# Normalisation and half of the offsets at a feed-forward's entry: from ScalarE to VectorE

## The chip, the core and the metric

The kernel runs on one core of a Trainium2 chip. The metric is the time of one execution on the device in microseconds, the median of several runs. In what follows PE is TensorE (PEld its weight loads), DVE is VectorE, ACT is ScalarE, POOL is GpSimd and SP the queue that issues most transfers. L200 is line 200 of the kernel before; the changed kernel's lines stand three or four further down in the parts that matter (L405 of before is L408 of after).

## What is computed

Two layers of an encoder over 512 tokens of 1024 channels, each a half-step feed-forward, a mixer of four groups of attention heads, and another half-step feed-forward, with a layer norm behind each:

```python
alpha = (2 * DEPTH) ** 0.25
for l in range(DEPTH):
    x = _layer_norm(alpha * x + 0.5 * _swiglu(x, ffn_w_gu[l, 0], ffn_w_down[l, 0]), ln_g[l, 0], ln_b[l, 0])
    mix = _token_mixers(x, w_in[l], ...)
    x = _layer_norm(alpha * x + mix, ln_g[l, 1], ln_b[l, 1])
    x = _layer_norm(alpha * x + 0.5 * _swiglu(x, ffn_w_gu[l, 1], ffn_w_down[l, 1]), ln_g[l, 2], ln_b[l, 2])
```

`_layer_norm` subtracts the mean, multiplies by 1 / sqrt(variance + 1e-5), then applies a gain and an offset for each channel. `_swiglu(h)` is (silu(h W_gate) * (h W_up)) W_down with 2816 inner columns. All is float32.

## The kernel before

The tokens are handled in four blocks of 128 (t = 0 to 3). Every float32 matrix product is made of three products of rounded operands: each operand is split into a high part (a copy in the rounded type, made on ACT) and a low part (the operand less its high part, made on DVE), and high x high, high x low and low x high are added up in PSUM.

The gate and up products of a feed-forward use a 2x2 block scheme with seven products instead of eight. It wants sums and differences of the blocks of both operands. On the side of x these are al1 to al7, each of 8 x 256 turned values (channels by tokens), each again as a high and a low part. Blocks 0 and 1 of the tokens give al1 and al2; blocks 2 and 3, combined with what was kept of 0 and 1, give al5, al7, al6, al4 and al3, by way of the differences t5, t7, t6 and t3 (L216, L218, L220, L225). On the side of the weights, the columns come in pairs (`Pair`). A pair has a step for each product: step 1 (al1, PSUM tile ga) and step 2 (al2, gb), then `rest`: step 5 (al5, gc), 6 (al6, ga), 7 (al7, ga), 3 (al3, gc) and 4 (al4, ga). Its weight sums are made in place on DVE: b11+b12 (L458), t2 (L468), b12+b22 (L476) and b21+t2 (L491); `parts4` then splits a sum or a weight into wh (ACT, L404) and wl (DVE, L405).

`norm_to_al` is the entry to a feed-forward. It runs three times: at the end of the mixer of layer 0, at the seam between the layers (after the second feed-forward of layer 0), and at the end of the mixer of layer 1. For each block it adds the accumulated product to x (L349), takes the statistics (L350, L331), forms the factor 1 / sqrt on DVE and POOL (L333, L334), forms minus mean times factor on DVE (L352), and normalises the block's two halves of 128x512 on ACT (L354), as factor times x plus that. Then `to_al` turns the block: PE transposes it (L112) into two PSUM tiles xtp of four 128x128 pieces, g = 0 for the lower 512 channels and g = 1 for the upper. In the turned x a channel is a partition, so `whole` applies the layer norm's gain and offset with one ACT operation for each piece (L200), eight for a block. For blocks 0 and 1 the results are kept (ac) and split at once into al1 (g = 0) and al2 (g = 1), by ACT (L181) and DVE (L182) with the sign turned; for blocks 2 and 3 they are t7 (g = 0) and a22 (g = 1), from which t5 and the rest follow (splits on L178, L179, L181, L182). The x that is not turned gets its gain and offset later, out of the way (`gain_later`).

A PSUM tile xtp comes free when its four pieces have been read, and there are two of them.

The order on each engine is made by a scheduler from priorities; the normalisation stands at a raised priority (`tc.high_priority(NORMS)`). Each engine then runs its own list in order, and waits on semaphores where an operand or a buffer is not ready.

Of the kernel before, what the change touches and what calls it, by code (L numbers as in the profile page):

```python
# [14 lines left out]
AF = mybir.ActivationFunctionType  # L15
ALU = mybir.AluOpType
# [57 lines left out]
def tile_encoder(ctx: ExitStack, tc: tile.TileContext, d: dict, out: bass.AP):  # L74
    nc = tc.nc
    ve, se, ge, te = nc.vector, nc.scalar, nc.gpsimd, nc.tensor
# [18 lines left out]
    def load(dst, src):  # L95
        nc.sync.dma_start(dst, src)
# [39 lines left out]
    def turned_x(t, gs=range(2)):  # L136

        for g in gs:
            b = bank4("pt", "xtp")
            for k in range(4):  # L140
                tr(b[:, k], x[t][:, (4 * g + k) * P:(4 * g + k + 1) * P])
            yield g, b
# [29 lines left out]
    def al_split(n, i, src, sign=1.0):  # L172

        for h, l, k0, nk in al[n]:
            cs = slice(i * P, (i + 1) * P)
            v = src[:, k0:k0 + nk]
            if sign == 1.0:
                se.copy(h[:, :, cs], v)  # L178
                ve.tensor_tensor(l[:, :, cs], v, h[:, :, cs].bitcast(F32), op=ALU.subtract)  # L179
            else:  # L180
                se.activation(h[:, :, cs], v, AF.Copy, scale=sign)  # L181
                ve.scalar_tensor_tensor(l[:, :, cs], v, sign, h[:, :, cs].bitcast(F32), op0=ALU.mult, op1=ALU.subtract)  # L182

    def b4(tag, name):
        return block(tag, name).rearrange("p (t c) -> p t c", c=P)

    def to_al(t, gt=None, gs=range(2)):


        i = t % 2  # L190

        def whole(g, b, tag, name):

            o = b4(tag, name)
            if gt is None:
                se.copy(o, b)
                return o, o
            for k in range(4):
                kk = 4 * g + k
                se.activation(o[:, k], b[:, k], AF.Identity, bias=gt[:, 1, kk:kk + 1], scale=gt[:, 0, kk:kk + 1])  # L200
            return o, o

        if t < 2:
            for g, b in turned_x(t, gs):
                kept[g, i], b = whole(g, b, "hl", "ac")
                al_split(1 + g, i, b, -1.0)
            return
        turned = list(turned_x(t))
        a22, b1 = whole(*turned[1], "tb", "a22")
        if gt is None:  # L210
            b0 = turned[0][1]
            t7 = b4("tb", "t7")
        else:
            t7, b0 = whole(*turned[0], "tb", "t7")
        t5 = b4("tb", "t5")
        ve.tensor_tensor(t5, b0, a22, op=ALU.subtract)  # L216
        al_split(5, i, t5)
        ve.tensor_tensor(t7, b0, kept[0, i], op=ALU.subtract)  # L218
        t6 = kept[0, i]
        ve.tensor_tensor(t6, t6, t5, op=ALU.subtract)  # L220
        al_split(6, i, t6)
        al_split(7, i, t7)
        al_split(4, i, b1, -1.0)
        t3 = kept[1, i]
        ve.tensor_tensor(t3, t3, t6, op=ALU.subtract)  # L225
        al_split(3, i, t3)
# [71 lines left out]
    def gain_tiles(l, i, tags=("hl",) * 4):  # L298

        out_ = []  # L300
        for n in range(2):
            for w in ("ln_g", "ln_b"):
                t = block(tags[len(out_)], w)
                load(t, d[w][l, i, n * FD:(n + 1) * FD].partition_broadcast(P))
                out_.append(t)
        return out_
# [22 lines left out]
    def norm_factors(stt):  # L329
        mv = sm.tile([P, 2], F32, tag="mv", name="mv", bufs=2)  # L330
        ve.bn_aggr(mv, stt)  # L331
        rs = sm.tile([P, 2], F32, tag="rs", name="rs", bufs=2)
        ve.tensor_scalar(rs[:, 0:1], mv[:, 1:2], 1.0, EPS * INV_A * INV_A, op0=ALU.mult, op1=ALU.add)  # L333
        ge.tensor_tensor(rs[:, 1:2], rs[:, 0:1], mhalf[:, 0:1], op=ALU.pow)  # L334
        return rs, mv
# [3 lines left out]
    def norm_to_al(t, accs, c, l, i):  # L339

        if t == 0:
            gt = sm.tile([P, 2, 8], F32, tag="gt", name="gt", bufs=1)
            load(gt, d["ln_t"][l, i])
            gained[:] = [gt]
        with tc.high_priority(NORMS):
            stt = sm.tile([P, 2, 6], F32, tag="bn", name="bn", bufs=2)
            xs = [x[t][:, n * FD:(n + 1) * FD] for n in range(2)]
            for n in range(2):
                ve.scalar_tensor_tensor(xs[n], accs[n], c * INV_A, xs[n], op0=ALU.mult, op1=ALU.add)  # L349
                ve.bn_stats(stt[:, n], xs[n])  # L350
            rs, mv = norm_factors(stt)
            ve.tensor_scalar(rs[:, 0:1], mv[:, 0:1], rs[:, 1:2], -1.0, op0=ALU.mult, op1=ALU.mult)  # L352
            for n in range(2):
                se.activation(xs[n], xs[n], AF.Identity, bias=rs[:, 0:1], scale=rs[:, 1:2])  # L354
        to_al(t, gained[0])

        if t == NT - 1:
            gained.append(gain_tiles(l, i, ("tb", "tb", "tb", "hl")))
# [478 lines left out]
    def mixer(l):  # L837
# [795 lines left out]
        def finish(t, accs):  # L1633
            norm_to_al(t, accs, 1.0, l, 1)
# [24 lines left out]
    for l in range(DEPTH):  # L1659
        ffn(l, 0, False, (new_xT, to_xT), ("p", "oT" if l else "nat"))  # L1660
        mixer(l)
        ffn(l, 1, l == DEPTH - 1, (norm_to_al,) if l < DEPTH - 1 else None)
# [24 lines left out]
```

## Time and profile before

| what | value |
|---|---|
| timed runs | 1926.14 us median of 3 (1925.88 to 1926.17) |
| the profiled execution | 1928.49 us, of which the span is 1926.7 us |
| mean granted TensorE clock | 0.988 |
| normalisations on ACT (L354) | 24 of 128x512 |
| offsets on ACT (L200) | 96 of 128x128, of which 48 write ac |
| L352 on DVE | 12 |
| entry at the mixer's end, layer 0 | about 607 to 648 us |
| entry at the seam between the layers | about 955 to 994 us |
| entry at the mixer's end, layer 1 | about 1560 to 1601 us |

A profile shows when each engine was busy. An engine's idle time matters only where another engine waits for its result, so the shares of the whole span say less than the windows of single stages. "x<-y" in a row names the tile written and the tiles read; a duration is that of one operation, and since operations in a queue overlap, the distance from start to start can be shorter.

### The profile page before, as it was taken

The numbers are of one execution on the slowest core, as the hardware profiler recorded it, in microseconds if no ns is written. First come the engines' busy times: TensorE is split into PE (matmuls) and PEld (weight loads), VectorE is DVE, ScalarE is ACT, GpSimd is POOL, SyncE is SP. The second block draws the span as 40 slices with busy tenths as digits, with TensorE's granted clock in tenths as the row PEclk, the third lists the DMA queues.
The fourth block names the chain that finished last, engine by engine and source line by source line (L and its number), as shares of the span: only waits on it lengthen the run. The fifth ranks groups of instructions, "written<-read, shape, count | busy, mean of one in ns | idle before, by whom it ended". The sixth has DMA issues, their size and how long they took to land.

```text
span 1926.7 us, 32397 instructions
## 1 busy us (share of the span) xinstructions
PE 1875.4 (97%) x12252; PEld 1704.4 (88%) x12252; DVE 1696.6 (88%) x2739; ACT 1061.6 (55%) x1851; POOL 251.6 (13%) x381
## 2 busy tenths in 40 slices
PE   7999999999999999999999999999999989999998
PEld 7999998888887899999789999988887879999996
DVE  7999995858988999999599999958689989999975
ACT  5555554248776645555375555532587865455551
POOL 0000000245731000000000000002467300000001
PEclk9999999999999999999999999999999999999999
DMA  6333314243343424233342333241533335144221
GB/s 231 107 121 108 102 52 136 81 121 99 93 105 110 138 94 131 84 104 112 108 133 80 106 99 121 65 144 52 144 92 84 102 110 170 50 132 131 64 91 66
DMA packets 164701, 205.65 MB, mean 107 GB/s; under 512 B 15360, under 2 KB 123904, under 8 KB 164544
## 3 DMA queue, kind: packets, MB, share of 16 engines
q1 hardware_dynamic: 164544, 203.57, 34.3%
q8 instruction: 97, 1.59, 0.3%
q14 instruction: 60, 0.49, 0.1%
HBM read 178.49 MB, written 2.10 MB: 94 GB/s over the span
## 4 chain that ended last, share of the span: by engine, by line
PE 63%; DVE 9%; ACT 2%; POOL 1%; DMA 1%; issue 1%; SPq 0%; DVEq 0%; POOLq 0%; ACTq 0%
PE ga L266 19%; PE gc L266 9%; PE acc L266 7%; PE da L266 5%; PE gb L266 4%; PE nat L266 3%; PE sc L266 3%; PE dc L266 3%; PE pjt L266 2%; PE ptb L112 2%; PE pv L266 2%; PE db L266 1%; DVE p L766 1%; DMA b<-in_ffn_w_gu_dram 1%; PE op L266 1%
## 5 line engine op out<-in xcount | busy, mean ns | idle before, releaser
L404 ACT CAST wh<-b 128x1024 fp32r<-128x1024 f32 x292 | 303.8, 1051 | 255.2 <-DVE b L468 61.1
L266 PE MATMUL ga<-al,wh 128*128 128x256 f32 x2752 | 389.7, 284 | 2.9 <-DVE al L179 1.7
L266 PEld LDWEIGHTS ga<-al,wh 128*128 128x128 f32 x2752 | 357.2, 191 | 14.2 <-ACT u L472 7.0
L405 DVE TENSOR_TENSOR wl<-b,wh 128x1024 fp32r<-128x1024 f32 x292 | 351.8, 1217 | 3.3 <-ACT wh L404 3.0
L266 PE MATMUL ga<-al,wl 128*128 128x256 f32 x1376 | 222.4, 284 | 5.4 <-DVE wl L405 5.3
L334 POOL TENSOR_TENSOR rs<-rs,mhalf 128x1 f32<-128x1 f32 x24 | 21.6, 901 | 1457.0 <-DVE rs L333 1449.0
L266 PE MATMUL gc<-al,wh 128*128 128x256 f32 x1408 | 203.5, 286 | 6.5 <-ACT al L178 5.1
L266 PEld LDWEIGHTS ga<-al,wl 128*128 128x128 f32 x1376 | 190.4, 193 | 6.4 <-DVE wl L405 6.4
L266 PEld LDWEIGHTS gc<-al,wh 128*128 128x128 f32 x1408 | 187.2, 195 | 9.5 <-ACT al L178 5.5
L541 ACT CAST wh<-d 128x512 fp32r<-128x512 f32 x168 | 98.5, 619 | 87.8 <-PE ga L266 39.2
L239 DVE TENSOR_TENSOR wl<-wr,wh 128x1024 fp32r<-128x1024 f32 (+2 forms) x50 | 59.4, 1188 | 78.5 <-ACT wh L238 78.5
L266 PE MATMUL acc<-wl,hh 128*128 128x512 f32 x320 | 125.3, 392 | 0.2 <-DVE wl L239 0.2
L266 PE MATMUL acc<-wh,hl 128*128 128x512 f32 x320 | 125.0, 390 | 0.0
L266 PE MATMUL acc<-wh,hh 128*128 128x512 f32 x320 | 124.9, 390 | 0.0
L266 PE MATMUL gc<-al,wl 128*128 128x256 f32 x704 | 117.0, 286 | 1.3 <-DVE wl L405 1.3
L238 ACT CAST wh<-wr 128x1024 fp32r<-128x1024 f32 (+2 forms) x50 | 50.9, 1025 | 121.9 <-PE acc L266 76.1
L542 DVE TENSOR_TENSOR wl<-d,wh 128x512 fp32r<-128x512 f32 x168 | 109.7, 683 | 0.1
L266 PE MATMUL da<-wh,dh 128*128 128x512 f32 x384 | 103.9, 392 | 0.0
L266 PEld LDWEIGHTS gc<-al,wl 128*128 128x128 f32 x704 | 99.6, 195 | 1.7 <-DVE wl L405 1.7
L808 ACT CAST pth<-ptb 128x512 fp32r<-128x512 f32 (+2 forms) x128 | 69.7, 545 | 43.0 <-PE ptb L112 41.9
L266 PE MATMUL gb<-al,wh 128*128 128x256 f32 x640 | 90.7, 285 | 0.0
L811 DVE TENSOR_TENSOR ptl<-ptb,pth 128x512 fp32r<-128x512 f32 (+2 forms) x128 | 80.6, 630 | 7.0 <-ACT pth L808 6.6
(323 smaller groups left out, 4157.9 us busy)
## 6 DMA issues: line engine op xcount, KB each, us to landing
b<-in_ffn_w_gu_dram SPq DMA_DIRECT2D x176, 512.0 KB, 4.6
d<-in_ffn_w_down_dram SPq DMA_DIRECT2D x96, 256.0 KB, 3.5
wr<-in_ffn_w_down_dram SPq DMA_DIRECT2D x40, 512.0 KB, 3.3
wr<-in_w_in_dram SPq DMA_DIRECT2D x30, 512.0 KB, 3.8
k<-ph SPq DMA_DIRECT2D x64, 128.0 KB, 2.3
wr<-in_w_out_dram SPq DMA_DIRECT2D x16, 512.0 KB, 3.2
qs<-ph SPq DMA_DIRECT2D x32, 128.0 KB, 2.4
ln_g<-in_ln_g_dram SPq DMA_DIRECT2D x14, 256.0 KB, 3.8
```

The source lines that it names most:

```text
L112: te.transpose(o, a, ident)
L238: se.copy(h[:, w], r[:, w])
L239: (lo or ve).tensor_tensor(l[:, q], r[:, q], h[:, q].bitcast(F32), op=ALU.subtract)
L266: te.matmul(o, a, b, start=start, stop=stop, **kw)
L334: ge.tensor_tensor(rs[:, 1:2], rs[:, 0:1], mhalf[:, 0:1], op=ALU.pow)
L404: se.copy(h, r[:, q])
L405: ve.tensor_tensor(lo, r[:, q], h.bitcast(F32), op=ALU.subtract)
L541: se.copy(wh[:, sl], self.r[rn][q])
L542: ve.tensor_tensor(wl[:, sl], self.r[rn][q], wh[:, sl].bitcast(F32), op=ALU.subtract)
L766: ve.tensor_tensor_reduce(p, sb, nd, -h.slope, h.sink[0] if h.sink else 3.0e38, ALU.add, ALU.min, m)
L808: se.copy(b.ph, b.tb[:, b.k0:b.k1])
L811: ve.tensor_tensor(b.pl, b.tb[:, b.k0:b.k1], b.ph.bitcast(F32), op=ALU.subtract)
```

## The change

In `norm_to_al` the L352 of DVE and the two L354 of ACT are replaced by two operations on DVE, x less mean, times factor, with both as scalars by pointer. In `whole` the pieces of g = 1 get their gain and offset from a DVE operation with two scalars by pointer; those of g = 0 stay on ACT.

```diff
@@ -197,7 +197,11 @@
                 return o, o
             for k in range(4):
                 kk = 4 * g + k
-                se.activation(o[:, k], b[:, k], AF.Identity, bias=gt[:, 1, kk:kk + 1], scale=gt[:, 0, kk:kk + 1])
+                gain, offset = gt[:, 0, kk:kk + 1], gt[:, 1, kk:kk + 1]
+                if g:
+                    ve.tensor_scalar(o[:, k], b[:, k], gain, offset, op0=ALU.mult, op1=ALU.add)
+                else:
+                    se.activation(o[:, k], b[:, k], AF.Identity, bias=offset, scale=gain)
             return o, o
 
         if t < 2:
@@ -349,9 +353,8 @@
                 ve.scalar_tensor_tensor(xs[n], accs[n], c * INV_A, xs[n], op0=ALU.mult, op1=ALU.add)
                 ve.bn_stats(stt[:, n], xs[n])
             rs, mv = norm_factors(stt)
-            ve.tensor_scalar(rs[:, 0:1], mv[:, 0:1], rs[:, 1:2], -1.0, op0=ALU.mult, op1=ALU.mult)
             for n in range(2):
-                se.activation(xs[n], xs[n], AF.Identity, bias=rs[:, 0:1], scale=rs[:, 1:2])
+                ve.tensor_scalar(xs[n], xs[n], mv[:, 0:1], rs[:, 1:2], op0=ALU.subtract, op1=ALU.mult)
         to_al(t, gained[0])
 
         if t == NT - 1:
```

For each entry that is 8 operations of 128x512 and 16 of 128x128 that leave ACT's queue and enter DVE's, and 4 of 128x1 that leave DVE's. Over the kernel DVE has 2802 instructions instead of 2742 and ACT 1606 instead of 1678; PE's, POOL's and SP's numbers stay. The scheduler also puts others elsewhere. Three places of the first entry show it. In the rows, a name's number tells one buffer from another, and the sizes are those of the output.

First, DVE from the low halves of the second block's al2 to the first operations on the third block. Before:

```order
L182 SCALAR_TENSOR_TENSOR al2_6956<-ac_7070,al2_6955 128x2x128
L182 SCALAR_TENSOR_TENSOR al2_6958<-ac_7070,al2_6957 128x2x128
L216 TENSOR_TENSOR t5_7126<-t7_7121,a22_7116 128x512
L218 TENSOR_TENSOR t7_7121<-t7_7121,ac_7001 128x512
L220 TENSOR_TENSOR ac_7001<-ac_7001,t5_7126 128x512
L179 TENSOR_TENSOR al5_6948<-t5_7126,al5_6948 128x4x128
L225 TENSOR_TENSOR ac_7015<-ac_7015,ac_7001 128x512
L454 TENSOR_TENSOR s1_7264<-gb_7274,s1_7264 128x512
L179 TENSOR_TENSOR al6_6949<-ac_7001,al6_6949 128x4x128
L179 TENSOR_TENSOR al7_6950<-t7_7121,al7_6950 128x4x128
```

After (L202 is the new operation for g = 1, L220 and L222 are L216 and L218 of before, L408 is L405, L457 is L454, L461 is L458):

```order
L202 TENSOR_SCALAR ac_7068<-xtp_7063,gt_6981 128x128 x4
L182 SCALAR_TENSOR_TENSOR al2_6956<-ac_7068,al2_6955 128x2x128
L408 TENSOR_TENSOR wl_7301<-b11_7296,wh_7300 128x1024
L182 SCALAR_TENSOR_TENSOR al2_6958<-ac_7068,al2_6957 128x2x128
L202 TENSOR_SCALAR a22_7113<-xtp_7108,gt_6981 128x128 x4
L408 TENSOR_TENSOR wl_7332<-b21_7298,wh_7331 128x1024
L220 TENSOR_TENSOR t5_7123<-t7_7118,a22_7113 128x512
L461 TENSOR_TENSOR b11_7219<-b11_7219,b12_7223 128x1024
L179 TENSOR_TENSOR al5_6948<-t5_7123,al5_6948 128x4x128
L222 TENSOR_TENSOR t7_7118<-t7_7118,ac_7000 128x512
L457 TENSOR_TENSOR s1_7260<-gb_7270,s1_7260 128x512
L224 TENSOR_TENSOR ac_7000<-ac_7000,t5_7123 128x512
```

The offsets of the second and third block (ac, a22) now run in DVE's queue ahead of t5; two of the wl splits of the second pair and the sum b11+b12 of the first pair stand here, where before the splits stood further down and the sum further up.

Second, DVE behind the fourth block's al6. Before:

```order
L179 TENSOR_TENSOR al6_6949<-ac_7056,al6_6949 128x4x128
L225 TENSOR_TENSOR ac_7070<-ac_7070,ac_7056 128x512
L405 TENSOR_TENSOR wl_7367<-b11_7223,wh_7366 128x1024
L179 TENSOR_TENSOR al3_6960<-ac_7070,al3_6959 128x2x128
L179 TENSOR_TENSOR al3_6962<-ac_7070,al3_6961 128x2x128
L405 TENSOR_TENSOR wl_7400<-t2_7397,wh_7399 128x1024
L405 TENSOR_TENSOR wl_7431<-b12_7227,wh_7430 128x1024
L405 TENSOR_TENSOR wl_7460<-b22_7229,wh_7459 128x1024
L405 TENSOR_TENSOR wl_7491<-b21_7225,wh_7490 128x1024
L458 TENSOR_TENSOR b11_7300<-b11_7300,b12_7524 128x1024
```

After (L471, L479 and L494 are L468, L476 and L491 of before):

```order
L179 TENSOR_TENSOR al6_6949<-ac_7054,al6_6949 128x4x128
L179 TENSOR_TENSOR al3_6960<-ac_7068,al3_6959 128x2x128
L179 TENSOR_TENSOR al3_6962<-ac_7068,al3_6961 128x2x128
L471 TENSOR_TENSOR t2_7393<-b11_7219,b22_7225 128x1024
L479 TENSOR_TENSOR b12_7223<-b12_7223,b22_7225 128x1024
L494 TENSOR_TENSOR b21_7221<-b21_7221,t2_7393 128x1024
L408 TENSOR_TENSOR wl_7396<-t2_7393,wh_7395 128x1024
L408 TENSOR_TENSOR wl_7427<-b12_7223,wh_7426 128x1024
L408 TENSOR_TENSOR wl_7456<-b22_7225,wh_7455 128x1024
L408 TENSOR_TENSOR wl_7487<-b21_7221,wh_7486 128x1024
L461 TENSOR_TENSOR b11_7296<-b11_7296,b12_7520 128x1024
```

The three sums t2, b12+b22 and b21+t2, which before were made among the normalisations of the blocks, now stand here, behind all splits of x and ahead of the wl splits that use them; the wl split of b11 has gone from here to a place ahead of the fourth block.

Third, ACT at the same place. Before:

```order
L404 CAST wh_7399<-t2_7397 128x1024
L178 CAST al7_6950<-t7_7193 128x4x128
L178 CAST al6_6949<-ac_7056 128x4x128
L404 CAST wh_7430<-b12_7227 128x1024
L404 CAST wh_7459<-b22_7229 128x1024
L178 CAST al3_6959<-ac_7070 128x2x128
L178 CAST al3_6961<-ac_7070 128x2x128
L485 ACT_TABLE_LOAD
L485 ACTIVATE s1_7264<-s1_7264 128x512
L485 ACTIVATE s1_7333<-s1_7333 128x512
L404 CAST wh_7490<-b21_7225 128x1024
L463 COPY p5_7395<-gc_7370 128x512
```

After (L466 is L463 of before, L407 is L404):

```order
L178 CAST al5_6948<-t5_7194 128x4x128
L178 CAST al7_6950<-t7_7189 128x4x128
L178 CAST al6_6949<-ac_7054 128x4x128
L178 CAST al3_6959<-ac_7068 128x2x128
L178 CAST al3_6961<-ac_7068 128x2x128
L466 COPY p5_7391<-gc_7366 128x512
L407 CAST wh_7395<-t2_7393 128x1024
L407 CAST wh_7426<-b12_7223 128x1024
L407 CAST wh_7455<-b22_7225 128x1024
L407 CAST wh_7486<-b21_7221 128x1024
```

All four casts wh of the first pair stood ahead of the copy of gc to p5, three of them among the al casts; now all four stand behind that copy.

## The prediction

> **What bounds the kernel now.** I read the page first, then the windows of the three entries that the change touches, the waits in them, and their timelines.
>
> ```profile
> span 1926.7 us, 32397 instructions
> PE 1875.4 (97%) x12252; PEld 1704.4 (88%) x12252; DVE 1696.6 (88%) x2739; ACT 1061.6 (55%) x1851; POOL 251.6 (13%) x381
> ```
>
> PE is busy for 97% of the span, so elsewhere nothing can be won on ACT or DVE. The windows (columns: us; busy time of PE, PEld, DVE, ACT, POOL with counts; granted clock; DMA share; GB/s) show the exceptions: the mixer's end in layer 0, the seam between the layers, the mixer's end in layer 1, and the first of these up to a row that I need below.
>
> ```profile
> 607.00:648.00 41.00, 33.71 (x210) 30.27 (x208) 35.22 (x63) 36.57 (x74) 3.41 (x3) 0.88 0.24 73
> 955.00:994.00 39.00, 36.05 (x233) 31.99 (x232) 32.34 (x58) 35.23 (x73) 2.46 (x4) 0.96 0.22 72
> 1560.00:1601.00 41.00, 33.93 (x216) 30.76 (x215) 34.35 (x60) 36.57 (x74) 3.41 (x3) 0.88 0.21 67
> 606.96:636.79 29.83, 24.11 (x151) 21.48 (x150) 24.05 (x50) 27.56 (x62) 3.41 (x3) 0.89 0.06 18
> ```
>
> At a mixer's end PE works 33.7 of 41 us, at a mean clock of 0.88, while ACT (36.6) and DVE (35.2) are both nearly full. The first and third window read alike, so I work out the first and count it twice. Its waits (waiting engine, tile and line, what it waits for, then total us, count, mean):
>
> ```profile
> PE xtp L112 <- ACT ac L200: 2.6, 1, 2.6
> PE ga L266 <- DVE wl L405: 2.1, 1, 2.1
> DVE t L216 <- ACT t L200: 2.4, 1, 2.4
> DVE rs L352 <- POOL rs L334: 1.3, 3, 0.5
> DVE al L182 <- ACT al L181: 1.1, 1, 1.1
> ```
>
> PE waits for ACT once and for DVE once. Neither engine alone paces this stage: whichever gets more work becomes the pacer.
>
> **The change: prices.** Rows of single operations (groups give lowest/median/highest ns, or busy us and mean ns; timeline rows give start and length):
>
> ```profile
> 607.21 1.52 ACT L354 ACTIVATE x<-x,rs 128x512 f32<-128x512 f32 x2 [8.40 <-DVE rs L352]
> 608.99 1.51 ACT L200 ACTIVATE ac<-xtp,gt 128x128 f32<-128x128 f32 x4 [0.26 <-PE xtp L112]
> L354 ACT ACTIVATE x<-x,rs x24: 797/813/821, 607.2 to 1574.1; 128x512 f32<-128x512 f32 x24
> L200 ACT ACTIVATE ac<-xtp,gt x48: 436/458/526, 609.0 to 1572.3; 128x128 f32<-128x128 f32 x48
> L702 DVE CAST v<-nat x32: 213/238/501, 372.0 to 1352.3; 128x128 fp32r<-128x128 f32 x32
> L1246 DVE TENSOR_TENSOR nat<-nat,cgq 128x128 f32<-128x128 f32 x8 | 2.3, 283 | 0.1
> L363 DVE TENSOR_TENSOR x<-x,ln_g 128x512 f32<-128x512 f32 x24 | 16.1, 682 | 0.0
> L480 DVE TENSOR_TENSOR p<-ga,p 128x512 f32<-128x512 f32 x44 | 30.2, 687 | 15.2 <-PE ga L266 14.7
> L333 DVE TENSOR_SCALAR rs<-mv 128x1 f32<-128x1 f32 x24 | 3.5, 145 | 0.2
> L352 DVE TENSOR_SCALAR rs<-mv,rs 128x1 f32<-128x1 f32 x12 | 2.6, 213 | 5.4 <-POOL rs L334 5.4
> 639.20 0.68 DVE L179 TENSOR_TENSOR al<-ac,al 128x512 fp32r<-128x512 f32 x1
> 639.80 0.68 DVE L225 TENSOR_TENSOR ac<-ac 128x512 f32<-128x512 f32 x1
> 643.34 3.49 DVE L405 TENSOR_TENSOR wl<-b,wh 128x1024 fp32r<-128x1024 f32 x3
> ```
>
> Operations in a queue overlap a little, so what counts is start to start. On ACT that is 1.52 - 0.81 = 0.71 us for an L354 and (1.51 - 0.46) / 3 = 0.35 for an L200. On DVE it is 0.60 for a two-tensor operation of 512 elements (639.20 to 639.80) and (3.49 - 1.22) / 2 = 1.14 for one of 1024 (1.22 is a single one below).
>
> ACT loses, in an entry, 8 L354 and 16 of its 32 L200: 8 x 0.71 + 16 x 0.35 = 11.3 us. DVE loses four L352, each worth 0.13 in the queue (974.00 to 974.13 below), 0.5 us. It gains 8 tensor_scalar of 128x512 and 16 of 128x128 out of PSUM, which the trace does not show; I bound them.
>
> The 128x512 one has one source in SBUF and two scalars by pointer. The cast of one source, 128x128, took 238 ns against 283 for two sources, so the data part of one source seems to run at about two elements where two sources run at one. Halving the data part of 0.60 gives 0.33; each pointer adds about 0.07 (L352 against L333: 213 - 145). So 0.39 to 0.46; I take 0.43. If the pace stays at one element it is 0.60 plus pointers, 0.70.
>
> The 128x128 one reads PSUM. Its data part is a quarter, 0.20 in all by the same slope, and two pointers bring it to 0.33; the cast's 0.22 is the low end. I take 0.30. L480 reads a PSUM bank at 687 ns and L363 reads SBUF at 682, so I add nothing for PSUM. [...]
>
> So DVE gains 8 x 0.43 + 16 x 0.30 - 0.5 = 7.7 us in a stage where it has 41 - 35.2 = 5.8 us of idle time.
>
> **The change: the path at a mixer's end.** The order moves as well. The three sums L468, L476 and L491 of the first pair, which filled DVE's gaps, now stand behind all of the fourth block's splits; one L405 (of the b11 sum) and one L454 stand ahead of them. These rows carry the walk, all of before:
>
> ```profile
> 606.96 0.21 DVE L352 TENSOR_SCALAR rs<-mv,rs 128x1 f32<-128x1 f32 x1
> 636.79 0.69 DVE L179 TENSOR_TENSOR al<-t,al 128x512 fp32r<-128x512 f32 x1
> 637.37 1.26 PE L266 MATMUL gc<-al,wh 128*128 128x256 f32 x8
> 642.36 1.91 PE L266 MATMUL gc<-al,wh 128*128 128x256 f32 x8
> 638.64 2.00 ACT L404 CAST wh<-b 128x1024 fp32r<-128x1024 f32 x2
> 645.31 0.58 ACT L463 COPY p<-gc 128x512 f32<-128x512 f32 x1
> 646.62 0.64 PE L266 MATMUL ga<-al,wl 128*128 128x256 f32 x4
> 647.10 0.88 PE L266 MATMUL gc<-al,wh 128*128 128x256 f32 x6
> 646.80 1.22 DVE L458 TENSOR_TENSOR b<-b,b 128x1024 f32<-128x1024 f32 x1
> ```
>
> Step one: from the first block's factors (606.96) to the low half of al5 of the fourth block (636.79), on which the first gc product waits, DVE is busy for 24.05 of 29.83 us. Afterwards the same stretch holds 24.05 - 3 x 1.14 (sums gone behind) - 0.5 + 3.4 + 4.8 + 1.14 (L405 come ahead) + 0.6 (L454) = 30.1 us. Some waiting stays: POOL's power still lies between L333 and the normalisation (three times 0.3 to 0.5), and the high half of al2 comes from ACT. I take 1.7 of the 5.8 us. That puts al5 at 606.96 + 30.1 + 1.7 = 638.8, 2.0 later, and gc's start at 639.4.
>
> Step two: PE has no other work to put there. The wait for wl (2.1) goes, because both L405 stand ahead, so gb is done several us earlier, and PE then stands idle before gc and runs it at the lower clock. Eight products took 1.26 us at 637.37 after steady work and 1.91 at 642.36 after pauses, 0.13 and 0.23 apiece with the tail of 0.3 left out. I take 0.20 for gc's 24: 4.8 us, to 644.2.
>
> Step three: the copy of gc on ACT now stands ahead of the cast of the sum t2 (L404), and three casts, each at half of the pair's 2.00 or a little less (0.95), run in a row behind it: copy done at 644.7, third cast at 647.5. PE's products of step 6 are mixed with three of step 3, which need that third cast, and then 19 remain at 0.12 (four in 646.62 to 647.10): 649.8. Before, the last of step 6 were those at 646.62, and step 3 began behind them at 647.10; afterwards three of its products, 0.4 us, are already done. **A mixer's end costs 649.8 - 647.1 - 0.4 = 2.3 us.** DVE reaches the second pair's L458 (646.80 before) later still: 2.0 + 3.4 for the sums - 1.7 for what went ahead = 3.7. But PE then has the first pair's 67 products left, 8 us, and I cost that at nothing; if that cover is gone, it is 3.7 - 2.3 = 1.4 us more for each.
>
> **The seam between the layers.** There PE feeds the blocks one after another, and only the last stretch is DVE's:
>
> ```profile
> 972.80 0.15 DVE L333 TENSOR_SCALAR rs<-mv 128x1 f32<-128x1 f32 x1
> 974.00 0.21 DVE L352 TENSOR_SCALAR rs<-mv,rs 128x1 f32<-128x1 f32 x1 [0.45 <-POOL rs L334]
> 974.13 0.68 DVE L218 TENSOR_TENSOR t<-t,ac 128x512 f32<-128x512 f32 x1
> 982.62 1.23 DVE L458 TENSOR_TENSOR b<-b,b 128x1024 f32<-128x1024 f32 x1 [0.53 <-DMA b<-in_ffn_w_gu_dram]
> 985.56 0.68 DVE L179 TENSOR_TENSOR al<-t,al 128x512 fp32r<-128x512 f32 x1
> 986.30 1.44 PE L266 MATMUL gc<-al,wh 128*128 128x256 f32 x7 [0.77 <-DVE al L179]
> ```
>
> From the last block's L333 to its al5 DVE gains two normalisations and four offsets, 0.86 + 1.2 - 0.13, and gives up waits of 0.45 and 0.53: gc comes about 0.9 later. With 0.3 for the lower clock I take **1.2 us**.
>
> The sum is 2.3 + 2.3 + 1.2 = 5.8 us. The profiled execution took 1928.49 us (its span of 1926.7 and 1.8 around it), 2.35 more than the median of the timed runs, 1926.14. Against it the forecast is 1934.3, against the median 1932.0. With the low prices (1.6 us less in an entry) the sum is about 2, with the high ones and 0.8 more of waiting about 9: 1928.2 to 1935.4.
>
> **Rivals.**
>
> Faster: ACT is the true pacer. For it speak PE's 2.6 us wait for L200 and DVE's 2.4 us for t, which both go with ACT's 11.3 us. If DVE's new operations fit into its waits, the 2.4 us come off each entry: 3 x 2.4 = 7.2, 1918.9. It decides where DVE's 30.1 us fall under 27.4, that is at 5.5 us for the 24 new operations instead of 8.2. Against it: that is under my low prices. [...] Chance 0.22.
>
> No change: low prices, nearly all waits gone, and the clock not lower; -3.85 to +3.85 us about 1926.1. Within 0.2%, 3.85 us, a measurement of this kernel can't be told from no change. Chance 0.22.
>
> Much slower: the 128x512 operation runs at one element. Then 8 x 0.27 = 2.2 us more at each mixer's end and 0.6 at the seam: 5.8 + 5.0 = 10.8, 1936.9. For it speaks that no single-source 128x512 row with pointers exists; against it the cast. [...] Chance 0.11.
>
> **The numbers.** The forecast has 0.45, the faster rival 0.22, no change 0.22, the one-element rival 0.11. Slower is 0.45 + 0.11 = 0.56. The range runs from the faster rival's value to the one-element case with its own 2 us on top: 1919 to 1939. The forecast's own range is 1928 to 1935.5.
>
> **What would show it.** In the profile after: the new 128x512 operation near 0.43 us apart and the 128x128 one near 0.30; ACT's busy time in the first window near 25 us, DVE's near 41; no wait of PE for L200 at 617.9; al5 of the fourth block some 2 us later; a long idle of PE before gc; a lower clock there; the casts behind the copy of gc. I am wrong if gc starts no later than before, or if DVE still waits for several us between 607 and 637.

## The result and the profile after

The changed kernel took 1941.02 us (median of 4 runs, 1938.91 to 1942.64), the kernel before 1926.01 (4 runs, 1925.83 to 1926.17): a ratio of 1.0079, 95% interval 1.0064 to 1.0094. It is 15.0 us slower. The forecast had the sign and most of the places, but only 5.8 us, and its range ended at 1939.

The page of the changed kernel first. Its profiled execution took 1938.91 us, the shortest of the four.

```profile
span 1937.1 us, 32389 instructions
PE 1873.3 (97%) x12252; PEld 1702.0 (88%) x12252; DVE 1719.1 (89%) x2799; ACT 1029.6 (53%) x1779; POOL 248.5 (13%) x381
```

DVE took on 22.5 us of work and ACT gave up 32. The windows of the three entries, columns as in the prediction:

```profile
607.00:648.00 41.00, 29.56 (x185) 26.20 (x184) 39.37 (x76) 25.33 (x49) 1.70 (x3) 0.88 0.22 70
955.00:994.00 39.00, 33.73 (x206) 29.12 (x205) 35.90 (x77) 21.67 (x44) 3.09 (x4) 0.95 0.22 70
1560.00:1601.00 41.00, 31.84 (x196) 27.94 (x195) 39.45 (x83) 21.27 (x44) 2.27 (x4) 0.92 0.20 65
```

At a mixer's end DVE is now full (39.4 of 41 us, 35.2 before), ACT has 25 us of work instead of 37, and PE works 29.6 us instead of 33.7. The two new operations, as groups (lowest/median/highest ns) and in the timeline, where the distance to the next start shows what they cost in the queue:

```profile
L357 DVE TENSOR_SCALAR x<-x,mv,rs x24: 539/544/549, 605.1 to 1576.4; 128x512 f32<-128x512 f32 x24
L202 DVE TENSOR_SCALAR ac<-xtp,gt x24: 355/402/409, 607.9 to 1578.4; 128x128 f32<-128x128 f32 x24
605.11 1.00 DVE L357 TENSOR_SCALAR x<-x,mv,rs 128x512 f32<-128x512 f32 x2
606.02 1.28 DVE L354 BATCH_NORM_STATS2 bn<-x 128x6 f32<-128x512 f32 x2
618.41 1.36 DVE L202 TENSOR_SCALAR ac<-xtp,gt 128x128 f32<-128x128 f32 x4
```

A normalisation costs (606.02 - 605.11) / 2 = 0.46 us, an offset (1.36 - 0.40) / 3 = 0.32: at the upper ends of what was forecast. They are paid in a queue that had 5.8 us to spare in the window before.

Now the first entry. An entry's cost is read against its own start, the first block's L333 (L337 in the changed kernel), since other stages shift the two executions against each other. Before, with the first row behind step 7 as the end:

```profile
606.14 0.14 DVE L333 TENSOR_SCALAR rs<-mv 128x1 f32<-128x1 f32 x1
650.90 0.40 PE L266 MATMUL gc<-al,wh 128*128 128x256 f32 x2
```

After, DVE, PE and ACT:

```profile
604.28 0.14 DVE L337 TENSOR_SCALAR rs<-mv 128x1 f32<-128x1 f32 x1
636.65 0.68 DVE L179 TENSOR_TENSOR al<-t,al 128x512 fp32r<-128x512 f32 x1
...
636.23 0.58 PE L270 MATMUL gc<-al,wh 128*128 128x256 f32 x1 [5.66 <-ACT al L178]
637.38 1.86 PE L270 MATMUL gc<-al,wh 128*128 128x256 f32 x7 [0.57 <-DVE al L179]
639.90 1.91 PE L270 MATMUL gc<-al,wh 128*128 128x256 f32 x8
643.93 1.22 PE L270 MATMUL ga<-al,wh 128*128 128x256 f32 x8 [1.62 <-ACT wh L407]
645.82 1.01 PE L270 MATMUL gc<-al,wh 128*128 128x256 f32 x3 [0.67 <-ACT wh L407]
...
650.04 1.27 PE L270 MATMUL gc<-al,wh 128*128 128x256 f32 x5
654.48 0.52 PE L270 MATMUL gc<-al,wl 128*128 128x256 f32 x3
...
642.34 0.58 ACT L466 COPY p<-gc 128x512 f32<-128x512 f32 x1 [2.46 <-PE gc L270]
642.83 1.05 ACT L407 CAST wh<-t 128x1024 fp32r<-128x1024 f32 x1
643.77 2.94 ACT L407 CAST wh<-b 128x1024 fp32r<-128x1024 f32 x3
```

From the start to the end of step 7 it took 650.90 - 606.14 = 44.8 us before and 654.48 - 604.28 = 50.2 after, when three more gc products (0.36 us) are already done: the entry costs 5.1 us. PE stands 5.7 us ahead of gc, then 1.6 and 0.7 for casts. Three windows, columns as above, show the clock that was granted meanwhile (the third number from the end):

```profile
635.00:641.70 6.70, 4.90 (x21) 4.60 (x22) 6.70 (x12) 3.13 (x6) 0.00 (x0) 0.50 0.54 164
641.80:645.10 3.30, 1.68 (x13) 1.31 (x11) 3.21 (x4) 2.76 (x4) 0.00 (x0) 1.00 0.82 263
645.20:652.00 6.80, 6.18 (x29) 6.18 (x30) 6.21 (x6) 3.04 (x4) 0.00 (x0) 0.50 0.73 220
```

It is low for gc, where eight products take 1.9 us. It is full again while PE waits 1.6 us for the first cast and runs the eight products at 643.93, in 1.2 us. Then it is low once more, from 645.2 to 652.0. The third entry, before and after, by the same two rows:

```profile
1558.99 0.14 DVE L333 TENSOR_SCALAR rs<-mv 128x1 f32<-128x1 f32 x1
1603.12 0.40 PE L266 MATMUL gc<-al,wh 128*128 128x256 f32 x2
```

```profile
1563.36 0.14 DVE L337 TENSOR_SCALAR rs<-mv 128x1 f32<-128x1 f32 x1
1613.59 0.52 PE L270 MATMUL gc<-al,wl 128*128 128x256 f32 x3
```

44.1 us against 50.2, less 0.36: 5.7 us. At the seam, the last block's L333 was at 972.80 and its al5 at 985.56 before (both rows stand in the prediction); step 6 then started at 990.65, and the wl split of the second pair stood ahead of L333:

```profile
969.93 1.23 DVE L405 TENSOR_TENSOR wl<-b,wh 128x1024 fp32r<-128x1024 f32 x1 [0.66 <-ACT wh L404]
990.65 1.12 PE L266 MATMUL ga<-al,wh 128*128 128x256 f32 x8
```

After:

```profile
976.69 0.14 DVE L337 TENSOR_SCALAR rs<-mv 128x1 f32<-128x1 f32 x1
976.75 1.21 DVE L408 TENSOR_TENSOR wl<-b,wh 128x1024 fp32r<-128x1024 f32 x1
...
991.58 0.68 DVE L179 TENSOR_TENSOR al<-t,al 128x512 fp32r<-128x512 f32 x1
997.09 1.12 PE L270 MATMUL ga<-al,wh 128*128 128x256 f32 x8
```

From L333 to step 6 it is 20.4 us instead of 17.9. L337 itself also comes 0.3 later: PE's last wait for a weight ahead of the seam ends at 947.33 before and 950.93 after, 3.6 apart, and the two rows are 3.9 apart. Together that is 2.8 us. The three entries make 5.1 + 2.8 + 5.7 = 13.6 us, close to the 15.0 of the timed runs. The profiled execution shows only 1937.1 - 1926.7 = 10.4 in all, because it got some 3 us back elsewhere: the first entry already starts 1.9 us sooner than before (604.28 against 606.14), behind a stretch between 520 and 560 us in which the two kernels' instructions are the same and the clock was not (before, then after):

```profile
520.00:560.00 40.00, 37.01 (x205) 31.63 (x205) 35.19 (x113) 30.66 (x88) 17.44 (x27) 0.91 0.29 77
```

```profile
520.00:560.00 40.00, 36.94 (x220) 30.79 (x220) 37.31 (x118) 32.49 (x92) 17.55 (x28) 1.00 0.32 84
```

### The profile page after: what moved, and what is told of

It reads as the page before. It is cut to its first block, busy times and chain, and to the rows that moved or that the text cites. A ratio compares the mean times of both kernels' runs of the same rounds, so it can differ in the third digit from the quotient of the medians.

```text
span 1937.1 us, 32389 instructions
## 1 busy us (share of the span) xinstructions
PE 1873.3 (97%) x12252; PEld 1702.0 (88%) x12252; DVE 1719.1 (89%) x2799; ACT 1029.6 (53%) x1779; POOL 248.5 (13%) x381
## 4 chain that ended last, share of the span: by engine, by line
PE 81%; DVE 11%; ACT 2%; POOL 2%; issue 1%; DMA 1%; SPq 0%; DVEq 0%; POOLq 0%; ACTq 0%
PE ga L270 26%; PE gc L270 13%; PE acc L270 10%; PE da L270 7%; PE gb L270 5%; PE nat L270 4%; PE dc L270 3%; PE sc L270 2%; PE pjt L270 2%; PE ptb L112 2%; PE pv L270 2%; PE db L270 2%; DVE p L769 1%; PE op L270 1%; PE xtp L112 1%
## 5 line engine op out<-in xcount | busy, mean ns | idle before, releaser
L407 ACT CAST wh<-b 128x1024 fp32r<-128x1024 f32 x292 | 303.8, 1051 | 251.6 <-DVE b L471 58.9
L408 DVE TENSOR_TENSOR wl<-b,wh 128x1024 fp32r<-128x1024 f32 x292 | 352.5, 1218 | 3.5 <-ACT wh L407 3.3
L270 PE MATMUL gc<-al,wh 128*128 128x256 f32 x1408 | 208.9, 291 | 23.0 <-ACT al L178 19.3
L270 PEld LDWEIGHTS gc<-al,wh 128*128 128x128 f32 x1408 | 191.4, 199 | 27.3 <-ACT al L178 20.1
```

Of the source, the lines that this page charges most:

```text
L270: te.matmul(o, a, b, start=start, stop=stop, **kw)
L407: se.copy(h, r[:, q])
L408: ve.tensor_tensor(lo, r[:, q], h.bitcast(F32), op=ALU.subtract)
```

## The experiments

Twelve kernels; each ratio is to the kernel before in the same session. First theory: DVE's queue sets an entry once its idle time is used up, and the low clock behind PE's pause adds to it. Rivals: the order in which the weight sums now stand; the place of the offsets (they hold PSUM tiles); ACT as the pacer.

### The two halves apart

Normalisation alone: the second hunk of the diff without the first.

> Only the normalisation goes to DVE; all 32 offsets of an entry stay on ACT. By the first theory (DVE's queue at an entry is what sets the time, and the low clock behind PE's pause adds to it) DVE gains 8 x 0.46 - 0.5 = 3.1 us in an entry where it had 5.8 us idle, so the fourth block's al5 comes no later than before or up to 1 us later, and the total lies 0 to 5 us above 1926. By the rival (what costs is the order in which the three weight sums now stand, not DVE's load) the two sums b12+b22 and b21+t2, which stand behind the splits here as well, cost as much as in the changed kernel: 8 us or more above 1926. By a second rival (ACT was the pacer, and its relief pays once DVE has room) 3 to 7 us below 1926.

Offsets alone: the first hunk without the second.

> Only the offsets of g = 1 go to DVE; the normalisation stays on ACT. By the first theory DVE gains 16 x 0.32 = 5.1 us in an entry, almost all of its 5.8 us of idle time, and the offsets sit where PE waits for a free PSUM tile: 5 to 11 us above 1926, more than with the normalisation alone. By the order rival the same as the normalisation alone, since the sums move alike. By the rival of ACT as the pacer, below 1926.

The normalisation alone took 1921.34 us, ratio 0.9973 (0.9964 to 0.9981): faster by 5 us. The offsets alone took 1929.67, ratio 1.0016 (1.0007 to 1.0024), 3 us slower. The halves make -0.11% together and the whole makes +0.79%: what costs is that both are there. The first theory had expected no gain from the normalisation and more loss from the offsets, 5 to 11 us; for the normalisation the second rival was right (ACT's relief pays while DVE has room). The order rival falls in the form that I gave it, since two of the sums stand behind the splits here too, at no loss. But t2, the sum that step 6 needs first, stands ahead of al5 here (at 631.04), so this run does not test its place. The window and the first entry of the normalisation alone:

```profile
607.00:648.00 41.00, 35.94 (x247) 32.70 (x246) 39.35 (x69) 31.82 (x67) 3.17 (x4) 0.96 0.28 82
```

```profile
607.07 0.14 DVE L333 TENSOR_SCALAR rs<-mv 128x1 f32<-128x1 f32 x1
634.20 0.39 PE L266 MATMUL gc<-al,wh 128*128 128x256 f32 x1 [2.03 <-ACT al L178]
634.32 0.69 DVE L179 TENSOR_TENSOR al<-t,al 128x512 fp32r<-128x512 f32 x1
635.06 1.25 PE L266 MATMUL gc<-al,wh 128*128 128x256 f32 x7 [0.48 <-DVE al L179]
636.97 1.91 PE L266 MATMUL gc<-al,wh 128*128 128x256 f32 x8
```

From L333 to al5's low half it is 27.3 us here, against 636.79 - 606.14 = 30.7 before and 636.65 - 604.28 = 32.4 with the offsets as well. In the window DVE is as busy as in the changed kernel (39.4), but between L333 and al5 it works 26.2 us, in the changed kernel 30.8; PE works 35.9 us in the window instead of 29.6. The 4.6 us between them are the offsets, 16 x 0.32 = 5.1, less t2's sum, which stands behind al5 in the changed kernel (1.14), and one L457 more (0.6). DVE also waits 0.5 us longer, and al5 comes 5.1 us later: what the offsets add to DVE goes to the path whole.

### The order of the sums

`early()` raises the priority of the first pair's four sums at an entry:

```diff
+                with self.early():
+                    ve.tensor_tensor(r[11], r[11], r[12], op=ALU.add)
...
+                with self.early():
+                    ve.tensor_tensor(r[21], r[21], r[6], op=ALU.add)
```

> The changed kernel, with the first pair's four sums at a raised priority, so that DVE makes them ahead of the fourth block's splits again. By the first theory the total of DVE's work ahead of step 6 is the same; al5 comes up to 2 us later and step 6 no sooner, and the time stays within 4 us of the changed kernel's 1941. By the order rival the time comes back to within 4 us of 1926.

1937.30 us, ratio 1.0057 (1.0045 to 1.0069). Some 4 us of the 15 come back, at the edge of what the theory allowed and of what the intervals can tell; three quarters stay. PE's rows of the first entry show what changed:

```profile
642.56 1.86 PE L270 MATMUL gc<-al,wh 128*128 128x256 f32 x7 [0.43 <-DVE al L179]
647.43 1.12 PE L270 MATMUL ga<-al,wh 128*128 128x256 f32 x8
```

The cast of t2 is done ahead of gc, so step 6 follows gc without a pause, and no second low stretch comes (eight products in 1.12 us). For that, gc's seven products start 36.5 us behind L337 (642.56 - 606.11) instead of 33.1 (637.38 - 604.28), since the sums stand ahead of al5 again. The place of t2 is worth some 4 us; most of the loss is there without it.

### The clock

```diff
+        def keep_busy(n):
+            o = bank("pv", "idle")
+            for _ in range(n):
+                mm(o[:, :256], alk(2, "h", 0)[:, :P], alk(2, "h", 0), True, True, skip_group_check=True)
...
+                if entry and not self.j:
+                    keep_busy(40)
                 self.c = self.bank("pj", "gc")
```

> The changed kernel, with 40 products that nobody reads put into PE's queue ahead of the first gc of an entry, where PE waits for 4 to 6 us; everything else stands as it stood. If the low clock behind that pause is what made the loss larger than forecast, gc's 24 products take 2.9 us instead of 4.9 and step 6 runs at the full clock: 2 to 3.5 us less in each entry, 1931 to 1936 in all. If the loss is DVE's queue alone, gc starts at the same time, step 6 waits for the same casts, and the time stays within 1.5 us of 1941.

With 44, and 14 more in front of step 6 (`keep_busy(14, 6)`; the second argument names the operand that is read, al6):

> The changed kernel with 44 products that nobody reads ahead of the first gc of an entry and 14 more between gc and step 6, so that neither pause of PE is a pause. If the low clock is what step 6 still loses with 40 ahead of gc alone (its 16 products behind the casts at 0.21 us each), a mixer's end gains another 1 to 1.5 us: 1934 to 1936.5. If the short second pause of 1.6 us costs only itself, the time stays at 1938. Either way DVE's queue keeps al5 and the casts where they are, so it doesn't come back to 1926.

1938.25 us, ratio 1.0059 (1.0047 to 1.0071), between what the two readings expected, and 1934.59, ratio 1.0043 (1.0029 to 1.0057), clear of the change's interval. In the first, PE's rows of the first entry:

```profile
630.84 4.96 PE L270 MATMUL idle<-al 128*128 128x256 f32 x40
637.82 1.10 PE L270 MATMUL gc<-al,wh 128*128 128x256 f32 x7 [0.77 <-DVE al L179]
639.51 1.91 PE L270 MATMUL gc<-al,wh 128*128 128x256 f32 x8
643.89 1.22 PE L270 MATMUL ga<-al,wh 128*128 128x256 f32 x8 [1.62 <-ACT wh L408]
```

In the second:

```profile
638.70 1.12 PE L270 MATMUL gc<-al,wh 128*128 128x256 f32 x8
640.14 1.84 PE L270 MATMUL idle<-al 128*128 128x256 f32 x14
...
646.01 1.91 PE L270 MATMUL ga<-al,wh 128*128 128x256 f32 x8
```

The first filler moves the low clock only from gc's start into its second half; both together keep gc at full pace, and one low stretch at 645 to 649 remains. PE has only been given unread work, and 0.79 - 0.43 = 0.36%, 6.9 us, come off: so much at least does the low clock cost the changed kernel at its entries. It is not a share of the 15 us as it stands, since the kernel before has low stretches at its own entries too (eight products in 1.91 us at 642.36), and that kernel was not run with fillers. The 8 us that stay are DVE's queue, the casts behind it, and what is left of the clock; these runs do not part them.

### DVE's load or the offsets' place

Half of the moved offsets only, `if g and t < 2` and `if g and t >= 2`:

> The normalisation on DVE, and the offsets of g = 1 on DVE for the token blocks 0 and 1 only; those of blocks 2 and 3 stay on ACT. DVE gets 8 x 0.32 = 2.6 us in an entry more than with the normalisation alone, and 2.6 less than in the changed kernel. By the theory of DVE's load: halfway between 1921 and 1941, and the same as with blocks 2 and 3, 1927 to 1935. By the rival of the place (PSUM tiles held back while the mixer's last products wait behind the transposes): 1936 or more, near the changed kernel.

> The normalisation on DVE, and the offsets of g = 1 on DVE for the token blocks 2 and 3 only. By the theory of DVE's load the same as with blocks 0 and 1, 1927 to 1935; the three sums stand behind the splits as in the changed kernel, so if that order is what costs, it is 1934 or more. By the rival of the place: 1921 to 1925, near the normalisation alone.

1930.43 us, ratio 1.0020 (1.0011 to 1.0028), and 1930.97, ratio 1.0026 (1.0016 to 1.0036): the same, and about halfway. The rival of the place falls, but the load is not proved by it, since the two come to the same time in different ways: at the first entry gc's seven products start 34.9 us behind L337 with blocks 0 and 1 (638.41 - 603.48) and step 6 follows without a pause; with blocks 2 and 3 they start after 30.3 us (633.98 - 603.73), and PE then waits 1.6 us for the cast of t2. Last, DVE's load without the offsets: the normalisation alone, with the statistics taken twice.

```diff
+                for _ in range(2):
                     ve.bn_stats(stt[:, n], xs[n])
```

> The normalisation alone on DVE, and each block's statistics taken twice over (the second time into the same tile, so nothing else changes): 8 x 0.60 = 4.8 us more on DVE in an entry, nearly what the offsets add (16 x 0.32 = 5.1), while all offsets stay on ACT. If DVE's load as such turns the gain into a loss, the time goes from 1921 to 1934 or more, most of the way to the changed kernel. If it is what the offsets do to ACT's queue and to the PSUM tiles, it rises by no more than 6 us, 1921 to 1927.

1936.07 us, ratio 1.0049 (1.0036 to 1.0061). 4.8 us of DVE work in an entry that is no offset and reads no PSUM turn a gain of 5 us into a loss of 9.5. Its first entry:

```profile
608.41 0.15 DVE L333 TENSOR_SCALAR rs<-mv 128x1 f32<-128x1 f32 x1
640.03 0.69 DVE L179 TENSOR_TENSOR al<-t,al 128x512 fp32r<-128x512 f32 x1
640.77 1.86 PE L266 MATMUL gc<-al,wh 128*128 128x256 f32 x7 [1.02 <-DVE al L179]
```

al5 comes 31.6 us behind L333 instead of 27.3, and gc runs at the low clock again. It is no test of load alone: the second statistics also stand in each block's own chain, ahead of its normalisation, and in this run the clock was low ahead of gc too: its mean from 607 to 648 is 0.83 (0.96 with the normalisation alone), at a low clock of 0.50 some 14 us, while from PE's pause ahead of gc (636.6) to 647.2, where the products are at full pace again, there are only 10.6. The versions without fillers, the sums on POOL apart, by what they add to DVE in an entry (0.46, 0.32 and 0.60 us for each operation, less 0.5 for the four L352 where they go):

| version | added to DVE, us | ratio to before |
|---|---|---|
| one half of the normalisation | 1.8 | 0.9970 (0.9959 to 0.9982) |
| normalisation | 3.2 | 0.9973 (0.9964 to 0.9981) |
| offsets | 5.1 | 1.0016 (1.0007 to 1.0024) |
| normalisation, offsets of blocks 0 and 1 | 5.7 | 1.0020 (1.0011 to 1.0028) |
| normalisation, offsets of blocks 2 and 3 | 5.7 | 1.0026 (1.0016 to 1.0036) |
| normalisation, statistics twice | 8.0 | 1.0049 (1.0036 to 1.0061) |
| the change, sums early | 8.3 | 1.0057 (1.0045 to 1.0069) |
| the change | 8.3 | 1.0079 (1.0064 to 1.0094) |

It turns between 3.2 and 5.1 us, below the 5.8 us that DVE had idle in the window before. The load does not tell all: at 8.0 and 8.3 us, where PE has no pause for the casts behind gc at the first entry, the loss is 0.49 and 0.57%; the change, with that pause, loses 0.79%.

### A miss: the sums on POOL

```diff
-                ve.tensor_tensor(r[11], r[11], r[12], op=ALU.add)
+                (ge if entry and not self.j else ve).tensor_tensor(r[11], r[11], r[12], op=ALU.add)
```

> The changed kernel with the first pair's four weight sums made on POOL instead of DVE. By the theory that DVE's load sets the entry, DVE gives up 4 x 1.14 = 4.6 us there; al5 comes about 1 us sooner (only b11+b12 stands ahead of it), step 6's operands 3 us sooner unless POOL needs over 3 us for a sum: 1929 to 1935. By the rival that the offsets hurt by their place (they hold the PSUM tiles that PE's transposes wait for), the sums don't matter: 1939 to 1942.

1946.91 us, ratio 1.0108 (1.0095 to 1.0121), slower still. It tells nothing about the load, since the sums ran ahead of the powers in POOL's queue:

```profile
606.97 2.33 POOL L495 TENSOR_TENSOR b<-b,t 128x1024 f32<-128x1024 f32 x1
609.26 0.55 POOL L338 TENSOR_TENSOR rs<-rs,mhalf 128x1 f32<-128x1 f32 x1
```

At 2.3 us and more each they held the first block's power back to 609.3, 3.3 us behind its L337, and every block behind it. Sums that start only behind the last power were not tried.

### Versions that beat both

```diff
+            ve.tensor_scalar(rs[:, 0:1], mv[:, 0:1], rs[:, 1:2], -1.0, op0=ALU.mult, op1=ALU.mult)
+            se.activation(xs[1], xs[1], AF.Identity, bias=rs[:, 0:1], scale=rs[:, 1:2])
+            ve.tensor_scalar(xs[0], xs[0], mv[:, 0:1], rs[:, 1:2], op0=ALU.subtract, op1=ALU.mult)
```

> One of a block's two halves is normalised on DVE, the other on ACT, side by side; all offsets on ACT. DVE gets 4 x 0.46 = 1.8 us in an entry (its 128x1 operation stays), ACT loses 4 x 0.71 = 2.8. By the theory that the emptier of the two queues should get the work, it lies between before and the normalisation alone: 1920 to 1925. If splitting a block shortens its way to PE by 0.4 us, it is better than the normalisation alone: below 1920.

1920.82 us, ratio 0.9970 (0.9959 to 0.9982), not to be told from the normalisation alone. With fillers, the normalisation alone:

> The normalisation alone on DVE, with 16 products that nobody reads in PE's queue at an entry, nine of them ahead of the first gc and seven in the earlier waits. PE waits there for 2.5 us and then ran one stretch of 3.4 us at the lower clock. If the clock is worth what it was in the changed kernel, 1.0 to 1.7 us come off each entry: 1916.5 to 1919. If the wait is too short to matter, or the fillers stand in the way, 1921 to 1923.

1918.85 us, ratio 0.9960 (0.9947 to 0.9972). And the split with fillers:

> The same split, with the 16 fillers, fourteen of them ahead of the first gc. Between 1 and 4 us below the split without them if the clock falls there without them; no difference if it doesn't.

1918.48 us, ratio 0.9956 (0.9943 to 0.9970): 8 us below before, and by the ratios 24 below the change. The two with fillers can't be told apart, and their gain over the same versions without fillers is inside or at the edge of the intervals. The window of the normalisation with fillers shows the clock:

```profile
607.00:648.00 41.00, 36.84 (x274) 33.84 (x272) 39.77 (x67) 31.75 (x67) 2.62 (x3) 1.00 0.30 93
```

## Why the prediction was wrong

It had the sign, the pacer and the chain. Two terms of its sum were too small: the products of step 6 at a mixer's end, which it put at the full clock, and the operations that the order moves at the seam.

- **Prices.** 0.43 and 0.30 us forecast, 0.46 and 0.32 measured. Right; the one-element rival's 0.70 is ruled out. No run shows apart what the pointers and the PSUM source add, so that the sum of both came out for the 128x128 one may be luck.
- **Step one at a mixer's end.** al5 was to come 2.0 us later; it came 32.4 - 30.7 = 1.7 later. The list of what stands ahead of al5 was right, and so were its 30.1 us of work and 1.7 of waiting: from the first L357 (605.11) to al5 DVE worked 30.0 us and was idle for 1.6.
- **Step two.** gc at 0.20 us a product, 4.8 us: from 637.38 to the copy at 642.34 it took 5.0. Right.
- **Step three failed.** "And then 19 remain at 0.12 [...]: 649.8." The casts stood where the forecast put them: its third one was to be done at 647.5, that is 645.6 once the 1.9 us are taken off by which this entry starts sooner, and PE's gc of step 3 starts at 645.82. But the 19 products then took 650.04 - 645.82 = 4.2 us, 0.22 each, not 2.3, and some nine more behind them took 2.0 us instead of 1.1. These 1.9 and 0.9 us are what parts 2.3 from 5.1. The forecast took the low clock for gc's price alone. It did end with gc, but there stand the pauses of 1.6 and 0.7 us for the casts, and the clock fell again, from 645.2 to 652.0. The granted clock was 0.50 in both low stretches, and both ended when PE had worked without a pause for over 4 us (637.4 to 641.7, 645.8 to 652.0). The first had begun at 634.9, in the 5.7 us that PE stood ahead of gc; the second came behind 3.3 us (641.8 to 645.1) in which PE was busy for 1.7. So 2.3 became 5.1 and 5.7, the latter because gc had run at the full clock in the third entry before (eight products in 1.12 us at 1595.94). Fillers, which give PE unread work and no other engine any, took 6.9 us off.
- **The seam.** Of 0.9 us for al5 the profile shows 2.1 from L333 on: the wl split at 976.75 (1.14) and an L457 (0.6) moved into the stretch, only the sum (1.14) left it, and the wait for POOL that I had struck out (0.45) stayed at 0.44. 0.9 + 1.14 + 0.6 - 1.14 + 0.45 is 2.0. I had counted new operations there and not the moved ones, which I had done for the mixer's end.
- **The rivals.** "ACT is the true pacer" was given as an alternative to DVE; it is the other side of the same balance. It is what happens with 1.8 or 3.2 us on DVE, and the change went past it.
- **The range** took in prices and waits on both sides, and no case in which the clock is low again in step 6. That case is worth 2.8 and 3.4 us at the two mixers' ends and the seam 1.6, together 7.8 of the 9.2 us that the forecast lacks; where the other 1.4 lie the profile, of the fastest execution, does not show.

## What to carry to other kernels

Where two engines share a stage and both are nearly full, moving work from one to the other can gain up to a point and then lose more than it gained. Count the receiver's idle time in that stage alone, and don't take all of it as usable: here 3.2 of 5.8 us gained and 5.1 lost, in this one kernel. Then move the half that fits. List what the scheduler has moved into and out of the stretch between the first block's start and the operand that PE waits for, sum it, and do so at each entry. And where a late operand makes PE pause, price what follows at the low clock too, and look whether a shorter pause behind it makes the clock fall again: at the entries of both kernels it stood at 0.50 for 3.4 or 6.8 us at a time, though not behind every pause (in the kernel before it was 1.00 behind the wait of 2.1 us that ended at 633.44).

## What the runs showed of the hardware

- With the normalisation alone, a pause of 2.0 us and another of 0.5, with one product between them, were followed by a low stretch (eight products in 1.91 us at 636.97). In the changed kernel a pause of 1.6 us was (low from 645.2 to 652.0). With nine unread products in the longer pause of the first, and seven in earlier ones, the clock was 1.00 for the whole window. A pause of 2 us can cost, then; each of these is one profiled execution.
- A tensor_scalar of 128x512 with two scalars by pointer took 544 ns and 0.46 us in the queue, two-tensor operations of that size 682 ns and 0.60. One of 128x128 out of PSUM took 402 ns and 0.32: for a quarter of the data, seven tenths of the cost.
